# Three weight products moved from the matmul engine to the vector engine, and the last expert's down product cut in two halves

## The chip, the cores and the metric

The kernel runs on one core of one Trainium2 chip. TensorE (PE in the profile; its weight loads are PEld) multiplies, VectorE (DVE) and ScalarE (ACT) do elementwise work, GpSimd (POOL) little, SyncE (SP) issues nearly all DMAs. The metric is the device time of one execution in microseconds; lower is better.

## The reference, cut to what matters

Two transformer layers over 256 latent and 256 context tokens, width 1024. Each layer has six modulation vectors (adaLN) made from the conditioning vectors, a mixer and a feed-forward: layer 0 a dense SwiGLU, layer 1 eight experts of which each latent token uses two. Only the latent tokens leave.

```python
for i in range(DEPTH):                                   # DEPTH = 2
    mod_x = split(silu(c) @ ada_w[i] + ada_b[i], 6)      # 1024 x 6144 weights a layer
    mod_c = split(silu(c_ctx) @ ada_w[i] + ada_b[i], 6)
    hx = rms(x, norm1_w[i]) * (1 + mod_x[1]) + mod_x[0]
    hc = rms(ctx, norm1_w[i]) * (1 + mod_c[1]) + mod_c[0]
    y_x, y_c = mixer(hx @ w_in[i], hc @ w_in[i])
    x = x + mod_x[2] * (y_x @ w_out[i])
    h = rms(x, norm2_w[i]) * (1 + mod_x[4]) + mod_x[3]
    x = x + mod_x[5] * ffn(h)        # i=0: (silu(h@wg) * (h@wu)) @ wd, width 2816, also for ctx
                                     # i=1: sum over the token's 2 of 8 experts, width 3584
return rms(x, final_norm_w)
```

Context tokens use layer 1 only as far as the mixer, so of layer 1's vectors for `c_ctx` only the first two are used.

## The kernel before

The stages follow one another: layer 0's projection and mixer (to about 290 us), the dense feed-forward (FFN, about 300 to 690), layer 1's projection and mixer (to 870), the router, then the eight experts (908 to 1733) and the final norm.

**adaLN vectors.** `ada_w` of a layer is cut into three parts of two vectors, and each part into 8 loads of 1 MB, each as two tiles `araw` of 128x1024 numbers. `ada()` (L193 to 230) multiplies them on PE: for every load a group of 8 matmuls of 32 rows by 256 columns (L214), four of them side by side in the array, with the two conditioning vectors as two columns of `cz`. `sums` transposes and adds at a part's end. `adas` is a generator of such groups. Three of its parts, (0,1), (0,2) and (1,0), are woven into layer 0's mixer and two, (1,1) and (1,2), into layer 1's, at steps fixed in a list; layer 0's first part has loads of its own (tile `a`).

**Dense products.** `gemm` streams weights `raw` (512 KB, 4 KB to a partition) through two buffers. ACT rounds each to `wh` (L149) and DVE makes the rest `wl` (L150), five buffers of each, and PE does three matmuls a product (L335 to L337, 24 for a load). In the FFN DVE further multiplies gate and up (`f`, L841) and makes the rest of the rounded product (`fl`, L845). The FFN runs through the gate and up units of its first half, a first down product (`down(0)`), the second half, and `down(1)`.

**Experts.** `Ahead` loads an expert's weights through 16 buffers of 1 MB (`rawe`), on SP's queue and in order: gate and up (rows of 8 KB and of 6 KB to a partition), then the down weights `md` (14 loads of 8 KB to a partition). The first 8 loads are issued when the last dense weight is. A load's buffer is free when PE has used it. The tokens of an expert are gathered into 96 slots (3 groups of 32; the third group is left out by a branch where it is empty, as it is in the last block). `down()` accumulates y in 32 rows for each column half and parity; `scatter()` adds the parities (yc, ye: L1139, L1141), multiplies by `g2`, splits into `yh` and `yl` (L1144 to L1146), and matmuls with the one-hot `oht` (L1153, L1154) put the rows back to their tokens, to be added to `xt` (L1155). A scatter runs inside the next expert's work; the last one has no next.

**End.** After the last scatter an `If` (L1360) repeats the experts where more than 96 tokens chose one. Behind it come squares of `xt` (L1380), `rsqrt` (13 instructions on 128x2), the scaling by the norm's weights (L1387) and four output DMAs.

Of the kernel before, what the change touches and what calls it, by code (L numbers as in the profile page):

```python
# [9 lines left out]
F32 = mybir.dt.float32  # L10
# [26 lines left out]
WARM = (16, 4)  # L37

UPS, DOWNS = (0, 4, 8), (0, 4, 6, 10, 14)

# [34 lines left out]
def tile_hybrid(ctx: ExitStack, tc, a, tap=None):  # L75
# [171 lines left out]

    def mod(layer, i, j):

        return mods[layer, i // 2][:, (i % 2) * 8:(i % 2) * 8 + 8, j]  # L250
# [82 lines left out]

    def mm3(out, wh, wl, hh, hl, first, last):
        pe.matmul(out, wh, hh, start=first, stop=False)  # L335
        pe.matmul(out, wh, hl, start=False, stop=False)  # L336
        pe.matmul(out, wl, hh, start=False, stop=last)  # L337
# [452 lines left out]
    def add_gated(layer, i, m, o, lo, hi):  # L790
        for c0, c1, j in HALVES:
            if lo <= c0 < hi:
                dve.scalar_tensor_tensor(x[m][:, c0:c1], o[:, c0:c1], mod(layer, i, j)[:, m:m + 1], x[m][:, c0:c1],
                                         op0=ALU.mult, op1=ALU.add)
# [33 lines left out]
    def ffn(acc):  # L828
        with tc.tile_pool(name="ff", bufs=1, reuse_waits="tile") as FF:
# [3 lines left out]
            def evac(key, o, *_):  # L833
# [7 lines left out]
                dve.tensor_mul(f, o, hold.pop(m))  # L841
                H = FF.tile([128, TOK], F32R, tag="fh", name="fh", bufs=15)
                L = FF.tile([128, TOK], F32R, tag="fl", name="fl", bufs=15)
# [14 lines left out]
            yield from gemm(gu[:FCUT], hp, evac, KT, head=HEAD, halves=True)  # L858
            yield from gemm(down(0), f_rhs[0], evac_d, 11)
            yield from gemm(gu[FCUT:], hp, evac, KT)  # L860
# [28 lines left out]
    g = mixer(0, M0, adas(lambda: mx.pool, (0, 1), (0, 2), (1, 0)))  # L889
# [33 lines left out]
    p, g = g, mixer(1, mixer_pool("mix1"), adas(lambda: mx.pool, (1, 1), (1, 2)))  # L923
# [7 lines left out]
    class Ahead:  # L931


        def __init__(self, blocks):
            self.src, self.t, self.n = [], [], 0
            for up, down in blocks:
                for st in range(2):
                    self.src += [(lambda up=up, w=w, st=st, k=k: up(w, st, k), 4 * SCS[st]) for w in range(2)
                                 for k in range(KT)]
                self.src += [(lambda down=down, c=c: down(c), 2048) for c in range(14)]  # L940

        def issue(self, upto):
            while len(self.t) < min(upto, len(self.src)):
# [4 lines left out]
                nc.sync.dma_start(t[:, 0:c], src())  # L948
# [19 lines left out]
    loader = Ahead([weights(lambda: 0)] + [weights(lambda p=p: turn_of[p - 1]) for p in range(1, NE)])  # L968
# [135 lines left out]
    def prepare(poscol):  # L1104
# [19 lines left out]
        for t in range(2):  # L1124
            dve.tensor_scalar(oh[:, t, :], iota[:, 0:SLOTS], poscol(t), None, op0=ALU.is_equal)
        p = ps("mm", name="ohT")
# [32 lines left out]

    def experts(blocks, load, first, flag=None):  # L1160
# [5 lines left out]
        def groups(b, body, zero, first):  # L1166
# [356 lines left out]
```

## Time and profile before

| what | value |
|---|---|
| median of 3 runs | 1763.3 us (1760.02 to 1767.48) |
| the profiled execution | 1758.96 us, its span 1757.2 us |
| mean granted TensorE clock | 0.993 |
| PE busy | 1691.4 us (96%) |
| DVE busy | 602.8 us (34%) |
| ACT busy | 443.0 us (25%) |
| read from HBM | 469.36 MB |

The span is what the engines' instructions take; the execution's own time is 1.8 us more. A busy PE counts matmuls that overlap, so that a share near 100% says that it always had work, not that it ran at its peak.

### The profile page before, as it was taken

Reading aid. Unit: us, or ns where it says so; the run is one execution under the profiler, and the core shown is the slowest. Engines: PE = TensorE matmul, PEld = TensorE weight load, DVE = VectorE, ACT = ScalarE, POOL = GpSimd, SP = SyncE. Lnnn points to the kernel's source line nnn. Section 1 sums busy time; section 2 is a strip of 40 time slices with the busy share of each in tenths; the row PEclk is TensorE's granted clock in tenths of the full one; section 3 lists DMA queues with packets and bytes.
Section 4 is the critical chain, followed back from the end, with each engine's and each line's share of the span. In section 5 each row is a group of like instructions: output and inputs, shape, how many; then the busy total and the mean of one; then the engine's idle time right before and its main releaser. Section 6 shows DMA issues by size and latency. Waiting matters only on the chain. (4 is left out here: it accounts for less than half of the span.)

```text
span 1757.2 us, 31023 instructions
## 1 busy us (share of the span) xinstructions
PE 1691.4 (96%) x13008; PEld 1001.2 (57%) x13008; DVE 602.8 (34%) x1400; ACT 443.0 (25%) x863; POOL 19.4 (1%) x42
## 2 busy tenths in 40 slices
PE   6999999999999999999999999999999999999985
PEld 4875557988888889876675434334343443333431
DVE  5734665733333336647441210201211021210213
ACT  4543553433222223455430100100110010100101
POOL 1000000000000000000000000000000000000000
PEclk9999999999999999999999999999999999999997
DMA  8435552233333323355499999999999999999993
GB/s 326 148 111 196 176 175 71 77 104 96 96 96 96 96 96 109 108 188 197 166 391 417 420 417 420 414 384 420 412 419 418 419 420 416 420 417 420 419 418 150
DMA packets 84860, 472.68 MB, mean 269 GB/s; under 512 B 9424, under 2 KB 9808, under 8 KB 52704
## 3 DMA queue, kind: packets, MB, share of 16 engines
q1 hardware_dynamic: 84240, 469.36, 68.7%
q8 instruction: 117, 1.92, 0.4%
q0 software_dynamic: 176, 0.56, 0.1%
q10 hardware_dynamic: 288, 0.52, 0.1%
q14 instruction: 39, 0.32, 0.1%
HBM read 469.36 MB, written 1.05 MB: 268 GB/s over the span
## 5 line engine op out<-in xcount | busy, mean ns | idle before, releaser
L1186 PE MATMUL up<-rawe,G 128*32 128x512 f32 (+1 forms) x5120 | 496.6, 540 | 3.8 <-PEq L1170 2.7
L1186 PEld LDWEIGHTS up<-rawe,G 128*32 128x32 f32 x5120 | 184.5, 110 | 301.9 <-issue 270.8
L335 PE MATMUL mm<-hh,wh 128*128 128x512 f32 (+1 forms) x856 | 305.6, 360 | 4.0 <-ACT hh L330 4.0
L336 PE MATMUL mm<-hl,wh 128*128 128x512 f32 (+1 forms) x856 | 304.5, 356 | 0.0
L337 PE MATMUL mm<-hh,wl 128*128 128x512 f32 (+1 forms) x856 | 303.5, 355 | 0.0
L1216 PE MATMUL y<-rawe,e 128*32 128x512 f32 x2240 | 255.0, 597 | 11.5 <-DMA rawe<-in_md_dram 7.0
L149 ACT ACTIVATE wh<-raw 128x1024 fp32r<-128x1024 f32 x120 | 127.1, 1059 | 324.7 <-PE mm L336 290.6
L150 DVE TENSOR_TENSOR wl<-raw,wh 128x1024 fp32r<-128x1024 f32 x120 | 146.7, 1223 | 175.0 <-ACT wh L149 172.4
L335 PEld LDWEIGHTS mm<-hh,wh 128*128 128x128 f32 x856 | 161.0, 189 | 31.6 <-ACT hh L330 5.2
L1216 PEld LDWEIGHTS y<-rawe,e 128*32 128x32 f32 x2240 | 82.2, 110 | 168.9 <-issue 147.5
L336 PEld LDWEIGHTS mm<-hl,wh 128*128 128x128 f32 x856 | 161.8, 189 | 27.4 <-issue 5.2
L337 PEld LDWEIGHTS mm<-hh,wl 128*128 128x128 f32 x856 | 161.7, 189 | 23.3 <-issue 1.6
L1259 DVE TENSOR_TENSOR hid<-sg,up 128x512 f32<-128x512 f32 (+1 forms) x48 | 27.0, 616 | 288.1 <-PE up L1186 288.1
L1241 ACT ACTIVATE e<-hT 128x256 f32<-128x256 f32 (+1 forms) x48 | 17.1, 358 | 395.3 <-PE hT L1238 394.5
L335 PE MATMUL mm<-fh,wh 128*128 128x512 f32 (+1 forms) x209 | 74.5, 356 | 0.0
L336 PE MATMUL mm<-fl,wh 128*128 128x512 f32 (+1 forms) x209 | 74.3, 355 | 0.0
L337 PE MATMUL mm<-fh,wl 128*128 128x512 f32 (+1 forms) x209 | 74.3, 355 | 0.0
L1242 DVE COPY e<-hT 128x256 f32<-128x256 f32 (+1 forms) x48 | 18.3, 391 | 132.9 <-ACT e L1241 132.7
L214 PE MATMUL ada<-araw,cz 128*32 128x256 f32 x640 | 54.6, 390 | 8.7 <-DMA araw<-in_ada_dram 8.1
L1141 DVE TENSOR_TENSOR ye<-y,yc 32x512 f32<-32x512 f32 x48 | 32.7, 682 | 71.3 <-ACT yc L1139 70.6
L1255 ACT ACTIVATE sg<-up 128x512 f32<-128x512 f32 (+1 forms) x48 | 22.8, 544 | 134.0 <-PE up L1186 134.0
L1121 DVE TENSOR_SCALAR G<-ga,scale,shift 128x96 f32<-128x96 f32 x32 | 11.8, 371 | 114.3 <-ACT G L1123 114.3
(292 smaller groups left out, 1389.6 us busy)
## 6 DMA issues: line engine op xcount, KB each, us to landing
rawe<-in_md_dram SPq DMA_DIRECT2D x112, 1024.0 KB, 18.1
rawe<-in_g_dram SPq DMA_DIRECT2D x64, 1024.0 KB, 20.1
rawe<-in_u_dram SPq DMA_DIRECT2D x64, 1024.0 KB, 19.8
raw<-in_ws_dram SPq DMA_DIRECT2D x120, 512.0 KB, 3.6
rawe<-in_g_dram SPq DMA_DIRECT2D x64, 768.0 KB, 15.9
rawe<-in_u_dram SPq DMA_DIRECT2D x64, 768.0 KB, 14.9
araw<-in_ada_dram SPq DMA_DIRECT2D x80, 512.0 KB, 4.5
a<-in_ada_dram SPq DMA_DIRECT2D x8, 1024.0 KB, 11.4
```

What stands on the lines that cost most here:

```text
L149: act.activation(h, raw, AF.Copy)
L150: dve.tensor_sub(l, raw, h)
L214: pe.matmul(o[32 * g:32 * g + 32, 0:256], cz[:, kt, 16 - 2 * row:48 - 2 * row], t[:, z:z + 256], start=(first and kt < 4), stop=(last and ...
L335: pe.matmul(out, wh, hh, start=first, stop=False)
L336: pe.matmul(out, wh, hl, start=False, stop=False)
L337: pe.matmul(out, wl, hh, start=False, stop=last)
L1141: dve.tensor_add(ye[32 * s:32 * s + 32, n * 512:(n + 1) * 512], y[s][32 * n:32 * n + 32, :], yc[32 * n:32 * n + 32, :])
L1186: last = pe.matmul(o[s][32 * c:32 * c + 32, 0:sc], g[:, k, 32 * s:32 * s + 32], w[k][:, c * sc:(c + 1) * sc], start=(k == 0), stop=(k == K ...
L1216: last = pe.matmul(y[s][r:r + 32, :], e[s][:, 2 * i + par, :], w[i][:, par * 1024 + n * 512:par * 1024 + (n + 1) * 512], start=(i == 0), s ...
L1242: dve.tensor_copy(e[s][:, 16 * st + h:16 * st + 4 * n, :], z[:, h:])
L1255: act.activation(sg[s], o[:, 0:SCS[st]], AF.Silu)
L1259: dve.tensor_mul(hid[st, s], sg[s], o[:, 0:SCS[st]])
```

## The change

Layer 1's three adaLN parts leave both mixers and are made in the FFN by `ada_beside`: 48 loads of 512 KB, for each a multiply-add on DVE into running sums of 128x1024 (two of them for the vectors that context uses, else one; the first of eight is a copy on ACT), and when a vector's 8 loads are done, three steps into the next vector, 4 matmuls of 32x256 per sum add over the partitions. A step stands behind each of 48 units of `gemm`.

The down weights are laid out anew, so that a load of the last expert holds 512 columns of four row tiles. For all other experts a load stays 1 MB but is two runs of 4 KB for a partition where it was one of 8 KB. The last expert's down product makes columns 0 to 511 from its first seven loads and 512 to 1023 from the other seven, in parts of at most two loads at the end. The first half's scatter, its addition to `xt` and its squares run inside the second half. y stays in 128 rows (four row tiles side by side), is multiplied by `g2` and split as it is, and the one-hot matrix, repeated four times, adds the four in the scatter. The final norm stands before the `If`, whose body computes it again.

```diff
+    def ada_beside(pool):
...
+        def total(v, sums):
+            for j, t in enumerate(sums):
+                r = 6 * j + v
+                for g in range(4):
+                    pe.matmul(o[32 * g:32 * g + 32, 0:256], oz[:, 16 - r:48 - r], t[:, g * 256:(g + 1) * 256],
+                              start=(r == 0), stop=(v == 5), tile_position=(0, 32 * g), skip_group_check=True)
+        load(0)
+        yield
+        load(1)
+        o = ps("ax", name="adav")
+        for i in range(6 * KT):
+            v, k = divmod(i, KT)
+            if k == 0:
+                sums = [pool.tile([128, D], F32, tag="asum", name="asum", bufs=4) for _ in range(2 if v < 2 else 1)]
+            w = raw.pop(i)
+            for j, t in enumerate(sums):
+                c = cz[:, k, 16 + j:17 + j]
+                if k == 0:
+                    act.activation(t, w, AF.Copy, scale=c)
+                else:
+                    dve.scalar_tensor_tensor(t, w, c, t, op0=ALU.mult, op1=ALU.add)
+            load(i + 2)
+            if k == 2 and v:
+                total(v - 1, before)
+            if k == KT - 1:
+                before = sums
+            yield
+        total(5, before)
...
+            vectors = ada_beside(FF)
...
+            for part in (first, gemm(down(0), f_rhs[0], evac_d, 11), gemm(gu[FCUT:], hp, evac, KT)):
+                for _ in part:
+                    with tc.issue_after(latest["dve"]), tc.issue_after(latest["pe"]):
+                        step(vectors)
+                    yield
...
-    g = mixer(0, M0, adas(lambda: mx.pool, (0, 1), (0, 2), (1, 0)))
+    g = mixer(0, M0, adas(lambda: mx.pool, (0, 1), (0, 2)))
...
-    p, g = g, mixer(1, mixer_pool("mix1"), adas(lambda: mx.pool, (1, 1), (1, 2)))
+    p, g = g, mixer(1, mixer_pool("mix1"), iter(()))
...
-                lambda c: a["md"][bass.ds(e(), 1), c].squeeze(0))
+                lambda c: a["md"][bass.ds(e(), 1), c // 2, :, :, c % 2].squeeze(0),
+                lambda c: a["md"][bass.ds(e(), 1), c % 7, :, c // 7].squeeze(0))
...
+LASTS = ((0, 4, 6, 7), (0, 2, 4, 6, 7))
+LAST_GROUPS = (2, 0, 1)
...
+        def down_last(b, e, finish):
+            for n in range(2):
+                y = [ps(("y", "mm")[n], name="y") for _ in range(3)]
+                w = {}
+                for i0, i1 in zip(LASTS[n], LASTS[n][1:]):
...
+                    groups(b, body, zero, i0 == 0, LAST_GROUPS)
+                    if n and i0 == 0:
+                        with tc.issue_after(behind[0]):
+                            finish(0, half)
+                    yield
+                half = split_last(y, n)
+            with tc.issue_after(behind[0]):
+                finish(1, half)
...
+    def split_last(y, n):
...
+        for i, s in enumerate(LAST_GROUPS):
+            dve.tensor_mul(u[s], y[s], g2[:, n * 512:(n + 1) * 512])
+            act.activation(h[s], u[s], AF.Copy)
+            for z in {0: (), 1: LAST_GROUPS[0:1], 2: LAST_GROUPS[1:]}[i]:
+                dve.tensor_sub(l[z], u[z], h[z])
...
+    def finish(n, half, oht, wcol):
...
+            if n and z == LAST_GROUPS[0]:
+                with tc.issue_after(last.ins):
+                    idle(WARM[2])
+        s = slice(n * 512, (n + 1) * 512)
+        for t in range(2):
+            dve.scalar_tensor_tensor(xt[:, t, s], p[t], wcol(t), xt[:, t, s], op0=ALU.mult, op1=ALU.add)
+            act.activation(xf[t][n], xt[:, t, s], AF.Square, accum_out=vn[:, t, n:n + 1])
+        for t in range(2):
+            dve.tensor_mul(xf[t][n], xt[:, t, s], fn[:, s])
```

Three places show how instructions move. The first is PE at the end of layer 1's mixer; `av` and `sc` are products of the mixer, `ada<-araw` the adaLN products, `mm` the next dense product. Before:

```order
L740 MATMUL av<-PT,vt_5760 64x256 x2
L740 MATMUL av<-PT,vt_5761 64x256 x2
L740 MATMUL av<-PT,vt_5762 64x256 x2
L715 MATMUL sc<-akz_5763,qa_5768 128x512
L214 MATMUL ada<-araw,cz 32x256 x8
L715 MATMUL sc<-akz_5764,qa_5768 128x512 x2
L335 MATMUL mm<-hh_89,wh 128x256
```

and there in the changed kernel:

```order
L803 MATMUL av<-PT,vt_5874 64x256 x2
L803 MATMUL av<-PT,vt_5875 64x256 x2
L803 MATMUL av<-PT,vt_5876 64x256 x2
L778 MATMUL sc<-akz_5877,qa_5882 128x512
L778 MATMUL sc<-akz_5878,qa_5882 128x512 x2
L398 MATMUL mm<-hh_89,wh 128x256
```

The rows of the mixer keep their order here, and the groups between them are gone. The second place is DVE in the FFN's first half, where `f` is the product of gate and up, `fl` its rest and `wl` the rest of a weight. Before:

```order
L841 TENSOR_TENSOR f<-mm,sg 128x512
L150 TENSOR_TENSOR wl<-raw,wh 128x1024
L845 TENSOR_TENSOR fl<-f,fh 128x512
L150 TENSOR_TENSOR wl<-raw,wh 128x1024
L841 TENSOR_TENSOR f<-mm,sg 128x512
```

and in the changed kernel, `asum` being the running sums:

```order
L904 TENSOR_TENSOR f<-mm,sg 128x512
L289 SCALAR_TENSOR_TENSOR asum<-araw,cz,asum 128x1024
L908 TENSOR_TENSOR fl<-f,fh 128x512
L289 SCALAR_TENSOR_TENSOR asum<-araw,cz,asum 128x1024 x3
L153 TENSOR_TENSOR wl<-raw,wh 128x1024 x2
L904 TENSOR_TENSOR f<-mm,sg 128x512
```

Between two `f`, which are two units of `gemm` apart, stand four multiply-adds more, and both `wl` follow them. The third place is DVE at the end of the last expert. Before:

```order
L1141 TENSOR_TENSOR ye<-y,yc 32x512 x6
L1144 TENSOR_TENSOR ye<-ye,g_7406 96x1024
L1146 TENSOR_TENSOR yl<-ye,yh 96x1024
L1155 SCALAR_TENSOR_TENSOR xt<-scat,wet,xt 128x512 x4
L1359 TENSOR_LOAD ovf
L1360 COMPARE_AND_BRANCH
```

and in the changed kernel, for the second half of the columns, `lu` being y times `g2` (the first, of the empty third group, depends on nothing late), `xf` the stream times the norm's weights and `fv` the sum of squares:

```order
L1257 TENSOR_TENSOR lu<-y,g_7308 128x512 x2
L1260 TENSOR_TENSOR yl<-lu,yl 128x512
L1257 TENSOR_TENSOR lu<-y,g_7308 128x512
L1260 TENSOR_TENSOR yh<-lu,lh 128x512 x2
L1279 SCALAR_TENSOR_TENSOR xt<-scat,wet,xt 128x512 x2
L1282 TENSOR_TENSOR xf<-xt,fn 128x512 x2
L1543 SCALAR_TENSOR_TENSOR fv<-vn,fv 128x2
```

Six additions of parities are gone, the rest is by 512 columns, and the product with the norm's weights stands ahead of the sum of squares. The branch of the `If`, before ahead of the norm, now stands behind it.

## Rows read from the trace of the kernel before

**Rows 1.** Windows: start:end, us, busy us (x) of PE, PEld, DVE, ACT, POOL; PEclk, DMA, GB/s

```profile
420.00:640.00 220.00, 220.00 (x972) 182.19 (x971) 73.83 (x84) 58.09 (x69) 0.00 (x0) 1.00 0.31 98
...
1000.00:1700.00 700.00, 691.78 (x6805) 270.86 (x6794) 112.77 (x208) 61.22 (x129) 0.00 (x0) 1.00 1.01 416
...
1733.00:1757.00 24.00, 5.02 (x18) 2.32 (x8) 14.20 (x29) 5.40 (x12) 0.00 (x0) 0.57 0.12 45
```

**Rows 2.** Windows, the three stretches with layer 1's adaLN products

```profile
225.00:270.00 45.00, 43.20 (x300) 22.48 (x299) 26.91 (x91) 23.85 (x74) 0.00 (x0) 1.00 0.51 175
760.00:800.00 40.00, 39.45 (x317) 28.59 (x315) 19.06 (x75) 17.78 (x41) 1.20 (x3) 1.00 0.69 236
800.00:862.00 62.00, 58.90 (x407) 33.77 (x406) 41.65 (x127) 35.25 (x90) 3.79 (x5) 1.00 0.52 169
```

**Rows 3.** Windows, the same stretches, tile araw alone: PE, PEld, PEclk, DMA, GB/s

```profile
225.00:270.00 45.00, 10.02 (x128) 2.62 (x128) 1.00 0.51 175
760.00:800.00 40.00, 8.44 (x106) 2.29 (x106) 1.00 0.69 236
800.00:862.00 62.00, 13.83 (x152) 3.58 (x150) 1.00 0.52 169
```

**Rows 4.** Timeline of PE in layer 0: start us, us, engine, line, instruction

```profile
134.39 0.40 PE L335 MATMUL mm<-hh,wh 128*128 128x512 f32 x1
134.71 0.64 PE L214 MATMUL ada<-araw,cz 128*32 128x256 f32 x8
135.28 0.50 PE L336 MATMUL mm<-hl,wh 128*128 128x512 f32 x1
```

**Rows 5.** Waits of all engines, 800 to 862: us in total, times, longest

```profile
ACT PT L731 <- PE pT L728: 10.8, 7, 3.0
...
PE ada L214 <- DMA araw<-in_ada_dram: 2.1, 5, 0.8
```

**Rows 6.** Waits of DVE in the FFN, 320 to 640

```profile
DVE wl L150 <- ACT wh L149: 103.8, 33, 4.2
DVE f L841 <- PE mm L337: 68.8, 21, 3.4
```

**Rows 7.** Lines of DVE, form by form: duration ns min/median/max

```profile
L150 DVE TENSOR_TENSOR wl<-raw,wh x120: 1206/1225/1227, 17.9 to 881.8; 128x1024 fp32r<-128x1024 f32 x120
...
L331 DVE SCALAR_TENSOR_TENSOR hl<-u,mod,hh x48: 470/479/486, 24.3 to 707.9; 128x256 fp32r<-128x256 f32 x48
...
L841 DVE TENSOR_TENSOR f<-mm,sg x22: 691/692/692, 347.3 to 628.8; 128x512 f32<-128x512 f32 x22
...
L1155 DVE SCALAR_TENSOR_TENSOR xt<-scat,wet,xt x32: 740/743/751, 1014.9 to 1744.5; 128x512 f32<-128x512 f32 x32
```

**Rows 8.** Windows: rows of 8 KB, of 6 KB, and mixer and dense weights (4 KB)

```profile
966.00:1028.00 62.00, 61.52 (x547) 23.99 (x543) 12.86 (x24) 7.12 (x14) 0.00 (x0) 1.00 1.01 419
...
1036.00:1058.00 22.00, 21.99 (x264) 9.03 (x260) 3.15 (x6) 2.41 (x6) 0.00 (x0) 1.00 1.02 417
...
797.00:799.00 2.00, 1.84 (x19) 1.23 (x18) 1.90 (x15) 0.02 (x1) 0.00 (x0) 1.00 1.03 406
```

**Rows 9.** Timeline of all engines from the last weight load on

```profile
1731.95 1.92 PE L1216 MATMUL y<-rawe,e 128*32 128x512 f32 x16 [0.54 <-SPq L1360]
...
1733.71 4.18 DVE L1141 TENSOR_TENSOR ye<-y,yc 32x512 f32<-32x512 f32 x6 [20.55 <-ACT yc L1139]
...
1742.37 2.88 DVE L1155 SCALAR_TENSOR_TENSOR xt<-scat,wet,xt 128x512 f32<-128x512 f32 x4 [0.89 <-PE scat L1154]
...
1743.84 0.63 PE L1154 MATMUL scat<-yl,oht 128*128 128x512 f32 x1
1745.82 0.63 ACT L1380 ACTIVATE fsq<-xt 128x512 f32<-128x512 f32 x1 [5.58 <-DVEq L1360]
...
1748.40 0.16 DVE L1381 TENSOR_TENSOR fv<-vn 128x2 f32<-128x2 f32 x1 [3.15 <-ACT fsq L1380]
...
1750.97 2.74 DVE L1387 SCALAR_TENSOR_TENSOR xt<-xt,fr,fn 128x512 f32<-128x512 f32 x4
```

More of the change, by code (lines that the diff above doesn't have):

```diff
@@ L336, in mm3 @@
         pe.matmul(out, wh, hl, start=False, stop=False)
-        pe.matmul(out, wl, hh, start=False, stop=last)
+        latest["pe"] = pe.matmul(out, wl, hh, start=False, stop=last).ins
     base = [0]
@@ L857, in ffn @@
             down = lambda i: [(0, (i, m)) for m in range(KT)]
-            yield from gemm(gu[:FCUT], hp, evac, KT, head=HEAD, halves=True)
-            yield from gemm(down(0), f_rhs[0], evac_d, 11)
-            yield from gemm(gu[FCUT:], hp, evac, KT)
+            vectors = ada_beside(FF)
+            first = gemm(gu[:FCUT], hp, evac, KT, head=HEAD, halves=True)
+            for _ in range(2 * KT):
+                next(first)
+                yield
[3 more added lines that the diff above has]
+                        step(vectors)
+                    yield
+            run(vectors)
             yield from gemm(down(1), f_rhs[1], evac_d, 11, head=HEAD, tail=TAILD)
@@ L931, in tile_hybrid, with __init__ @@
     class Ahead:
-        def __init__(self, blocks):
+        def __init__(self, blocks, halves=False):
             self.src, self.t, self.n = [], [], 0
-            for up, down in blocks:
+            for i, (up, down, half) in enumerate(blocks):
                 for st in range(2):
@@ L939, in __init__ @@
                                  for k in range(KT)]
+                down = half if halves and i == len(blocks) - 1 else down
                 self.src += [(lambda down=down, c=c: down(c), 2048) for c in range(14)]
@@ L1271, in experts @@
                 run(u)
-            y = [ps("y", name="y") for _ in range(3)]
-            u = down(b, y, e)
+            last = flag and b == len(blocks) - 1
+            if last:
+                u = down_last(b, e, lambda n, half: finish(n, half, oht, blocks[b][1]))
+            else:
+                y = [ps("y", name="y") for _ in range(3)]
+                u = down(b, y, e)
             step(u)
@@ L1279, in experts @@
                 with tc.issue_after(behind[0]):
[L1280 removed]
+                    nxt = prepare(blocks[b + 1][0], flag and b + 1 == len(blocks) - 1)
+                    if flag and b + 1 == len(blocks) - 1:
+                        with tc.issue_after(behind_oh[0]), tc.issue_after(behind_oh[1]):
+                            over.append(nc.values_load_multi_w_load_instructions(ovf[0:1, 0:1], min_val=0, max_val=1,
+                                                                                      bass_reorder=False)[1][0])
                     if flags:
@@ L1283, in experts @@
             run(u)
-            pending = scatter(y, oht, blocks[b][1])
-        run(pending)
+            pending = None if last else scatter(y, oht, blocks[b][1])
+        if pending:
+            run(pending)
     p1.close()
@@ L1299, in tile_hybrid, with xf_tiles @@
             act.activation(xt[:, t, :], ht[:, t, :], AF.Copy)
+    fn = XP.tile([128, D], F32, name="fn")
+    xf, over = [], []
+    def xf_tiles():
+        a_ = XP.tile([128, D], F32, tag="ye", name="xf", bufs=1)
+        xf[:] = [[a_[:, 0:512], a_[:, 512:]], [XP.tile([128, 512], F32, tag="yc", name="xf", bufs=2) for _ in range(2)]]
+    vn = RS.tile([128, 2, 2], F32, name="vn")
     post, wet = sm("post"), sm("wet")
```

144 lines of the change are left out of this document (109 added, 35 removed).

## The prediction

> **What bounds the kernel now.** I read the windows first, because the changed parts lie in stretches with different limits. In the FFN PE is busy for all of 420 to 640 us while DVE works a third of the time and DMA a third [rows 1]. From 1000 to 1700 the DMA share is 1.01 at 416 GB/s and PE is busy for 691.78 of 700 us: the experts' stream of weights sets the pace and PE is just fast enough [rows 1]. In the last 24 us PE works 5.02 us at a granted clock of 0.57, and a chain over DVE and ACT sets the end [rows 1]. So a microsecond saved on PE ahead of the experts brings the stream forward by a microsecond, one added to a weight load comes back many times, and the tail is worth what its chain becomes.
>
> Then I read the three stretches that lose work. PE is the busiest engine in each: 43.20 of 45, 39.45 of 40, 58.90 of 62 us [rows 2]. The adaLN products alone take 10.02, 8.44 and 13.83 us of it, 32.3 us for 384 of their matmul records, which are 48 groups of 8 [rows 3]. The timeline gives the same price by another way: with a group between them two dense matmuls stand 135.28 - 134.39 = 0.89 us apart [rows 4], without one 220/972 = 0.226 us [rows 1]; 0.66 us a group, 32 us for 48.
>
> **Part 1, PE in the mixers.** What of the 32.3 us is gained depends on what is next. From 760 to 800, DVE and ACT are busy 19.06 and 17.78 us of 40 [rows 2], well below what remains of PE (31 us): I take all 8.4 us. From 800 to 862, PE keeps 45.1 us and DVE has 41.65 [rows 2], and the chains between the engines are near: ACT waits 10.8 us for PE's transposes there, which then come earlier, and PE waits 2.1 us for the removed loads [rows 5]. I take 70% of 13.83, 9.7 us, with bounds of 4 and of 13.83 + 2.1. In layer 0, PE keeps 33.2 of 45 us against DVE's 26.91 [rows 2]: 70% of 10.02, 7.0 us, bounds 3 and 10. Three sums with six transposes, counted as slots of 0.226 us [rows 1], are 1.4 us (bounds 0 and 1.4). Together 26.5 us, bounds 16 and 36.
>
> **Part 1, PE in the FFN.** Eight sums of four matmuls of 32x256 are half a group of L214 each: 0.33 us, or 0.66 us if the entry to such a group is most of its price [rows 4]. With the two transposes behind ACT's copy at the end I take +5 us, bounds 3 and 8; PE has no slack there [rows 1], so this is paid in full. Net for both: -21.5 us, bounds -8 and -33.
>
> **Part 1, the work that hides.** 48 steps bring 56 multiply-adds of 128x1024 and 8 copies on ACT. One multiply-add is 479 ns at 256 and 743 ns at 512 elements [rows 7], so 743 + 2 x 264 = 1271 ns at 1024; `wl` with as many elements is 1225 [rows 7]. The tight place is the first 16 steps, with two sums. A unit is 24 matmuls, 5.43 us, so a pair of gate and up is 10.9 us of PE [rows 1]. DVE has for a pair `f` at 0.692, `fl`, counted like `f`, and two `wl` at 1.225 [rows 7]: 3.8 us; four multiply-adds add 5.1, so 8.9 of 10.9 us. It fits, and the waits agree: DVE stood idle 103.8 us for ACT's `wh` and 68.8 us for PE [rows 6], 172.6 us for 56 x 1.27 = 71 us. Queued behind a multiply-add are `fl` and the next `wl`; five buffers of `wl` stand between DVE and PE, 27 us of work. ACT has 58.09 busy of 220 us [rows 1], and 8 copies are nothing. The 48 loads stand on SP's queue among the dense weights'; with 512 KB each 5.43 us they add what the dense stream has, so the DMA share goes from 0.31 to some 0.62 [rows 1]. I cost all this at nothing; if the cover is gone, the third rival has the price.
>
> **Part 2, the down weights in runs of 4 KB.** 98 loads of seven experts change; the last expert's 14 are one run again. Rows of 8 KB move at 419 GB/s and rows of 6 KB at 417 [rows 8]. A fixed price for each run, through these two, puts 4 KB at 413 GB/s: 2.54 us for 1 MB instead of 2.50, +3.5 us for 98. The nearest row with 4 KB to a partition at a full share is 406 GB/s, over 2 us only [rows 8]: +7.9 us. The far bound is the FFN's dense stream, also 4 KB: 98 GB/s at a share of 0.31 [rows 1], 316 GB/s scaled up, which would be 3.32 us a load and +80 us. That stream has only two buffers and starts and stops, so I keep it for a rival and take +4 us, bounds 0 and 8.
>
> The Trainium skill, page "DMA: Bandwidth & Descriptors", section "Specifications", puts the smallest transfer that reaches full rate at 512 B; by that, runs of 4 KB would cost nothing, and the sum would be 4 us lower. The rows of 8 and 6 KB do not quite agree (419 and 417, both far above that size) [rows 8].
>
> **Part 2, the tail.** From the start of the last load's matmuls at 1731.95 to the span's end at 1757.2 are 25.25 us [rows 9]. The new chain, from that start: the matmuls take 1.92 us as before, the first group's being done at about 1.1. Then DVE has five operations of 128x512 in a row (two products with `g2`, three rests; that of the empty third group is early) at 0.69 us as `f` [rows 7]: to 4.6. Four scatter matmuls remain, 0.9 us at full clock: 5.5 (at the low clock, 0.63 us for each [rows 9], 7.1). Two additions to `xt` at 0.743 [rows 7]: 7.0. The last square, 0.63 us [rows 9], lies beside two products of 0.69 on DVE: 8.4. Twelve small operations at (1750.97 - 1748.40)/13 = 0.198 us [rows 9]: 10.8. Two scalings on each of ACT and DVE, 0.69 each: 12.2. The outputs then need what they need now, from 1753.71 to 1757.2 [rows 9]: 3.5 us, so 15.7. What goes is the parities (4.18), the 0.57 us between the last addition and the first square, three of four squares, and half of the scatter and additions [rows 9]. The first half's work, some 10 us of DVE, lies inside seven loads of 2.5 us. I take -9 us, bounds -6 and -11.
>
> **Sum.** -21.5 + 4 - 9 = -26.5 us on an execution of 1758.96 us, so 1732.5. That execution lies 4.3 us under the median of the runs; against 1763.3 I predict 1737 us.
>
> **The rivals.**
> 1. *The runs of 4 KB are slow*, which ends on the other side. A load takes 3.32 us as the dense stream suggests [rows 1]: -21.5 + 80 - 9 = +49.5, 1813 us. It decides from the point where a load takes 30.5/98 = 0.31 us more, a rate of 373 GB/s. Against it stand 417 and 406 [rows 8]. Chance 0.05.
> 2. *The mixers are bound by their chains*, not by PE: only the 8.4 us of 760 to 800 are gained, less 5 in the FFN. For it speaks DVE's 41.65 beside PE's 45.1 [rows 2]; against it, that ACT waits for PE there [rows 5]. -3.4 + 4 - 9 = -8.4, 1755 us. Chance 0.13.
> 3. *DVE becomes the bound in the first 16 steps*, if a multiply-add costs over (10.9 - 3.8)/4 = 1.76 us. At twice a `wl`, 2.45 us, a pair takes 13.6 us, and seven pairs (the others' are copies on ACT) 19 us more: 1756 us. The row of 743 ns for 512 speaks against it [rows 7]. Chance 0.05.
> 4. *The tail does not shrink* (the new scatter or the outputs wait for something that I do not see): 1746 us. Chance 0.10.
> 5. *All of the PE time comes back*, with the loads' waits, and runs of 4 KB cost nothing: -33 - 11 = -44, 1719 us. For it speaks a PE busy over 95% in all three stretches [rows 2]. Chance 0.10.
>
> **How the numbers follow.** My forecast has 0.57, with a range of its own of 1728 to 1746. The range of 1722 to 1755 takes in the fourth case and the near part of the others, and leaves out the first, half of the second, third and fifth: about 2 in 10. What a measurement can tell from no change is 0.5%, 8.8 us: faster is under 1754.5. Forecast, fourth and fifth case and a third of the second make 0.81, the rest of the second and the third 0.13; slower, the first case and what I may have missed of its kind, has 0.06.
>
> **What would show it.** Between 760 and 862 PE's busy time falls by 22 us, and the first expert product starts some 21 us earlier than 908; if it is under 10 earlier, the second case holds, and PE's waits in the mixer have grown. In the FFN PE stays at 100% and DVE rises by about 71 us; a PE that waits for `wl` is the third case. In a window of down loads at full share the rate reads 413 GB/s; under 373 is the first. From the last load's matmuls to the span's end are 16 us. I am wrong if the stream's start does not move with PE, if the rate under `md` falls, or if the tail has a new wait.

## The result, and the profile after

The changed kernel takes 1744.87 us (1743.95 to 1746.69, 4 runs) against 1765.22 us (1760.02 to 1767.48) for the kernel before: 0.9895, 95% interval 0.9875 to 0.9916, some 20 us faster. I had forecast 1737, 26 us faster.

The trace of one execution (1746.69 us, span 1744.8) answers to [rows 1] and [rows 2]. Windows, with the columns of those rows:

```profile
180.00:250.00 70.00, 61.93 (x382) 32.91 (x381) 41.31 (x147) 36.05 (x115) 0.00 (x0) 0.97 0.33 110
420.00:640.00 220.00, 220.00 (x1002) 179.09 (x1001) 114.99 (x129) 60.81 (x72) 0.00 (x0) 1.00 0.56 176
760.00:800.00 40.00, 37.26 (x259) 32.58 (x258) 26.47 (x90) 23.95 (x52) 2.41 (x5) 0.99 0.30 95
800.00:862.00 62.00, 58.07 (x339) 41.07 (x338) 40.39 (x132) 32.36 (x88) 3.13 (x5) 0.95 0.11 42
800.00:810.00 10.00, 9.66 (x30) 6.37 (x29) 7.98 (x21) 3.80 (x11) 2.60 (x4) 0.70 0.11 43
1000.00:1700.00 700.00, 684.57 (x6704) 265.56 (x6706) 111.03 (x211) 60.35 (x129) 0.00 (x0) 0.99 1.02 413
1728.00:1745.00 17.00, 3.59 (x15) 2.11 (x14) 7.52 (x22) 3.60 (x8) 0.00 (x0) 0.69 0.18 66
```

The first window has this row in the kernel before:

```profile
180.00:250.00 70.00, 66.12 (x455) 35.02 (x454) 44.00 (x157) 37.72 (x118) 0.73 (x1) 1.00 0.56 186
```

The reader sees three things. PE now has longer pauses in the mixers, and there the granted clock is below 1.00; in the kernel before it was 1.00 in every one of these mixer windows (this row and [rows 2]). In the FFN DVE has 41 us more to do in 220 us and PE still has no pause. In the experts' stream the rate is 413 where it was 416. DVE's wait for ACT's `wh` in the FFN, from 320 to 640, which answers to [rows 6], has shrunk from 103.8 us:

```profile
DVE wl L153 <- ACT wh L152: 45.1, 25, 4.2
```

Where each stage begins is read from three tiles. `xall` is first written where layer 0's mixer ends, `f` marks the FFN, `up<-rawe` the experts' up products (first to last) and `y<-rawe` their down products. First the kernel before, by tile (duration ns min/median/max, first and last start):

```profile
L793 DVE SCALAR_TENSOR_TENSOR xall<-mm,mod,xall x56: 473/478/485, 294.0 to 895.6; 128x256 f32<-128x256 f32 x56
L1186 PE MATMUL up<-rawe,G x5120: 482/550/617, 908.6 to 1697.8; 128*32 128x512 f32 x99, 128*32 128x384 f32 x98
L1216 PE MATMUL y<-rawe,e x2240: 589/592/1062, 961.8 to 1733.3; 128*32 128x512 f32 x187
```

then the changed kernel, the same tiles and lines:

```profile
L856 DVE SCALAR_TENSOR_TENSOR xall<-mm,mod,xall x56: 473/478/485, 289.9 to 879.8; 128x256 f32<-128x256 f32 x56
...
L904 DVE TENSOR_TENSOR f<-mm,sg x22: 691/692/692, 343.1 to 629.5; 128x512 f32<-128x512 f32 x22
...
L289 DVE SCALAR_TENSOR_TENSOR asum<-araw,cz,asum x56: 1273/1278/1282, 358.6 to 630.1; 128x1024 f32<-128x1024 f32 x56
...
L1310 PE MATMUL up<-rawe,G x5120: 482/550/617, 892.8 to 1688.0; 128*32 128x512 f32 x99, 128*32 128x384 f32 x98
...
L1370 PE MATMUL y<-rawe,e x224: 589/592/1061, 1689.6 to 1727.0; 128*32 128x512 f32 x112
```

| stage, from these rows (us) | before | after | change | forecast |
|---|---|---|---|---|
| to the first `xall` | 294.0 | 289.9 | -4.1 | -7.0 |
| first `xall` to first `up` | 614.6 | 602.9 | -11.7 | -14.5 |
| of that, first to last `f` | 281.5 [rows 7] | 286.4 | +4.9 | +5 |
| first to last `up` | 789.2 | 795.2 | +6.0 | +4 |
| last `up` to last `y` | 35.5 | 39.0 | +3.5 | 0 |
| last `y` to the span's end | 23.9 | 17.8 | -6.1 | -9 |

(-14.5 is 8.4 + 9.7 + 1.4 less 5.) The two traces are 12.4 us apart, the medians 20: the traced execution of the kernel before (1758.96) is shorter than all of its timed runs, and the changed one (1746.69) is the longest of its own. The experiments show where such differences arise.

The end of the changed kernel, timeline of all engines, which answers to [rows 9]:

```profile
1718.08 5.36 PE L1370 MATMUL y<-rawe,e 128*32 128x512 f32 x48
...
1725.71 1.92 PE L1370 MATMUL y<-rawe,e 128*32 128x512 f32 x16 [0.17 <-PEq L1294]
...
1726.84 0.69 DVE L1257 TENSOR_TENSOR lu<-y,g 128x512 f32<-128x512 f32 x1 [0.45 <-PE y L1370]
...
1731.22 1.41 DVE L1279 SCALAR_TENSOR_TENSOR xt<-scat,wet,xt 128x512 f32<-128x512 f32 x2 [1.04 <-PE scat L1272]
...
1734.02 0.15 DVE L1543 SCALAR_TENSOR_TENSOR fv<-vn,fv 128x2 f32<-128x2 f32 x1
...
1736.38 1.33 ACT L1551 ACTIVATE xf<-xf,fr 128x512 f32<-128x512 f32 x2 [3.00 <-DVE fr L336]
1736.38 0.88 DVE L1549 TENSOR_SCALAR xf<-xf,fr 128x512 f32<-128x512 f32 x2
1736.89 1.10 SPq L1552 DMA_DIRECT2D out_dram<-xf  x2
1737.13 0.95 ACTq L1552 DMA_DIRECT2D out_dram<-xf  x2
```

From the start of the last load's products the chain went as worked out: `xt` done at 6.9 us (7.0 in the sum), `fv` at 8.3 (8.4), the scaling's start at 10.7 (10.8) and end at 12.0 (12.2). But the outputs and the end then took 7.1 us, not 3.5. And the last `y` starts late for another reason than a load: PE's wait before it is 0.17 us, behind the branch that leaves out the empty third group (L1294).

One more thing made PE late in the last expert. With the first four loads it waits three times for a load, 1.32 to 1.43 us each, each time after 1.06 or 1.07 us of products. Below are the next 40 products, the window around them, and the same 40 products in the kernel before, where the waits are 1.34, 1.41 and 1.20 us and four short products with zeros stand ahead of the last:

```profile
1696.99 6.12 PE L1370 MATMUL y<-rawe,e 128*32 128x512 f32 x40 [1.42 <-DMA rawe<-in_md_dram]
1697.00:1703.00 6.00, 6.00 (x40) 1.38 (x40) 0.00 (x0) 0.00 (x0) 0.00 (x0) 0.72 1.00 418
...
1706.76 4.50 PE L1216 MATMUL y<-rawe,e 128*32 128x512 f32 x40 [1.20 <-DMA rawe<-in_md_dram]
```

The same 40 products take 1.6 us more at the lower clock.

### The profile page after: what moved, and what is told of

Read it like the earlier page. It is cut to its first block, busy times and chain, and to the rows that moved or that the text cites. A ratio compares the mean times of both kernels' runs of the same rounds, so it can differ in the third digit from the quotient of the medians.

```text
span 1744.8 us, 30522 instructions
## 1 busy us (share of the span) xinstructions
PE 1676.9 (96%) x12710; PEld 996.8 (57%) x12712; DVE 668.6 (38%) x1471; ACT 449.9 (26%) x874; POOL 19.4 (1%) x42
## 3 DMA queue, kind: packets, MB, share of 16 engines
q1 hardware_dynamic: 96784, 469.36, 69.7%
## 5 line engine op out<-in xcount | busy, mean ns | idle before, releaser
L1340 PE MATMUL y<-rawe,e 128*32 128x512 f32 x2016 | 228.8, 599 | 5.6 <-DMA rawe<-in_md_dram 4.2
L1340 PEld LDWEIGHTS y<-rawe,e 128*32 128x32 f32 x2016 | 74.2, 110 | 146.0 <-issue 132.1
L289 DVE SCALAR_TENSOR_TENSOR asum<-araw,cz,asum 128x1024 f32<-128x1024 f32 x56 | 70.5, 1278 | 0.0
L1244 DVE SCALAR_TENSOR_TENSOR xt<-scat,wet,xt 128x512 f32<-128x512 f32 x28 | 19.1, 745 | 79.5 <-PE scat L1243 79.5
```

The lines of the kernel that those rows point to most:

```text
L289: dve.scalar_tensor_tensor(t, w, c, t, op0=ALU.mult, op1=ALU.add)
L1244: dve.scalar_tensor_tensor(xt[:, t, s], p, wcol(t), xt[:, t, s], op0=ALU.mult, op1=ALU.add)
L1340: last = pe.matmul(y[s][r:r + 32, :], e[s][:, 2 * i + par, :], w[i][:, n * 1024 + par * 512:n * 1024 + (par + 1) * 512], start=(i == 0), s ...
```

## The experiments

**The first part alone.** The kernel before with `ada_beside`, nothing of the last expert.

```diff
-    g = mixer(0, M0, adas(lambda: mx.pool, (0, 1), (0, 2), (1, 0)))
+    g = mixer(0, M0, adas(lambda: mx.pool, (0, 1), (0, 2)))
...
+            vectors = ada_beside(FF)
...
-    p, g = g, mixer(1, mixer_pool("mix1"), adas(lambda: mx.pool, (1, 1), (1, 2)))
+    p, g = g, mixer(1, mixer_pool("mix1"), iter(()))
```

> Only the first part of the change: layer 1's adaLN vectors on VectorE in the FFN; down weights and the last expert as in the kernel before. In the changed kernel's trace the first expert product starts 15.8 us earlier than before (892.8 against 908.6). Theory: all of that comes from this part, so it starts there again and the end is 15 to 16 us earlier than in the kernel before, some 0.991 of its time, with the mixers' ends 4 us (layer 0) and 15 us (layer 1) earlier in sum and the FFN 5 us longer. Rival: part of it is owed to run-to-run differences, or the stream of expert weights gives it back; then the experts start earlier but the end moves by less than 8 us (0.996 or more).

1741.9 us, 0.9881 (0.9859 to 0.9902). Up products from 892.9 to 1682.2, so the stream takes 789.3 us, as before, and the last `y` comes 35.4 us after, as before. The first theory holds: all of the gain is here, and the rest of the change adds nothing to it (3 us less gain, if anything).

**The second part alone.**

```diff
+            last = flag and b == len(blocks) - 1
+            if last:
+                u = down_last(b, e, lambda n, half: finish(n, half, oht, blocks[b][1]))
...
+    o["md"] = np.ascontiguousarray(w).reshape(8, 7, 128, 2, 2, 1024)
```

(with all that belongs to these, and layer 1's products in the mixers as before)

> Only the second part: the down weights laid out anew and the last expert in halves; adaLN as before. Theory from the two traces: the seven down products with runs of 4 KB cost 6 us, the last expert's product 3.5 us more, the tail is 6 us shorter; in sum 3 us slower than before, a ratio of about 1.002. Rival, as the prediction had it: 4 us for the runs and 9 us off the tail, 5 us faster, 0.997.

1765.97 us, 1.0013 (0.9999 to 1.0027): no gain, as the first theory says, not 0.997. In its trace the stages of this part cost 8.1 us in the stream (797.3) and 3.1 before the last `y`, and give 7.3 behind it: 3.9 us lost, where the changed kernel loses 3.4. Its trace shows something else too: its front is that of the kernel before, yet `xall` starts at 296.6, not 294.0. PE's timeline there:

```profile
139.35 0.40 PE L340 MATMUL mm<-hh,wl 128*128 128x512 f32 x1
141.49 1.08 PE L217 MATMUL ada<-araw,cz 128*32 128x256 f32 x8 [1.75 <-DMA araw<-in_ada_dram]
142.50 0.80 PE L338 MATMUL mm<-hh,wh 128*128 128x512 f32 x1
143.10 0.63 PE L339 MATMUL mm<-hl,wh 128*128 128x512 f32 x1
...
145.09 0.39 PE L338 MATMUL mm<-hh,wh 128*128 128x512 f32 x1
```

An adaLN group waited 1.75 us for its load, and the matmuls behind it took 0.63 us instead of 0.40: the granted clock is 0.83 in the window from 140 to 150, against 1.00 in the kernel before. So this late load in layer 0's mixer cost its wait and then a stretch at the lower level of the clock, 1.2 GHz.

**The layout of the down weights alone.**

```diff
-                lambda c: a["md"][bass.ds(e(), 1), c].squeeze(0))
+                lambda c: a["md"][bass.ds(e(), 1), c // 2, :, :, c % 2].squeeze(0))
...
-    o["md"] = np.ascontiguousarray(w).reshape(8, 14, 128, 2048)
+    o["md"] = np.ascontiguousarray(w).reshape(8, 7, 128, 2, 2, 1024)
```

> The kernel before with nothing changed but the layout of the down weights: each load of all eight experts is two runs of 4 KB to a partition instead of one of 8 KB. Theory: the runs cost 0.05 us a load, so the time grows by 5 to 7 us (ratio 1.003 to 1.004) and windows within the down loads read 413 GB/s or a little less against 419 before. Rival: runs of 4 KB cost nothing (413 has another cause, such as waits for buffers), ratio 1.000. The rate of the FFN's dense stream would make 1.05.

1772.74 us, 1.0054 (1.0034 to 1.0075), some 10 us more, above the 5 to 7 of the theory. The stream takes 1709.8 - 915.3 = 794.5 us, 5.3 more than before. Its windows within down loads:

```profile
972.00:996.00 24.00, 23.69 (x208) 10.54 (x202) 3.60 (x12) 2.71 (x7) 0.00 (x0) 1.00 1.03 412
1184.00:1206.00 22.00, 22.00 (x237) 9.14 (x229) 1.67 (x4) 0.55 (x2) 0.00 (x0) 1.00 1.03 409
```

The share is 1.03, so the queue does not stand idle; the runs themselves are slower. Of the rest of this trace 6.7 us lie in front, where nothing was edited (`xall` at 298.4, `up` at 915.3, with a granted clock of 0.83 from 160 to 170), and 1.7 us between the last `up` and the last `y` (37.2 against 35.5). So of the 10 us 5.3, or 7.0 with the last expert, lie where the layout was changed.

**The kernel before once more,** without an edit.

> The kernel before, unchanged, for a second trace: its executions lie between 1759 and 1767 us, and the one shown is the fastest. Theory: they differ in the experts' stream (waits for loads, 1000 to 1733 us), while everything ahead of the first expert product at 908.6 repeats within 1 us. Rival: they differ in the front, or in the clock.

1758.83 us. `xall` starts at 294.2, `up` runs from 908.5 to 1697.7, the last `y` at 1733.2: within 0.2 us of the first trace. So these two traces do not tell why other executions take up to 1769 us. What the four traces with this front show together is that it differs ahead of the experts: `up` starts at 908.6, 908.5, 911.9 and 915.3 (mean 911.1) with layer 1's products in the mixers. With the products in the FFN seven traces (no filling, below) have 892.8, 892.9, 891.2, 891.8, 892.6, 893.3 and 888.9 (mean 891.9). The difference is 19.2 us, not 15.8; at `xall` it is 295.8 against 288.9, 6.9 us.

**Down weights held twice.** The first seven experts read runs of 8 KB from `md`, the last one its halves from a second copy, `md2`.

```diff
-                lambda c: a["md"][bass.ds(e(), 1), c // 2, :, :, c % 2].squeeze(0),
-                lambda c: a["md"][bass.ds(e(), 1), c % 7, :, c // 7].squeeze(0))
+                lambda c: a["md"][bass.ds(e(), 1), c].squeeze(0),
+                lambda c: a["md2"][bass.ds(e(), 1), c % 7, :, c // 7].squeeze(0))
```

> The changed kernel with the down weights held twice in memory: the first seven experts read them in runs of 8 KB as in the kernel before, the last expert in halves as in the change. Theory: the seven down products lose their 5.5 to 6 us again (792.4 us from the first to the last expert's up product become 786 to 787 by this trace's clock, as in the runs with the old layout), so the time is 5 to 7 us under the changed kernel's, about 1739 us, ratio 0.986 of before. Rival: the stream is slower for another reason than the runs (the last expert's structure, the clock), and the time stays at 1745, ratio 0.989.

1739.83 us, 0.9864 (0.9849 to 0.9879). (The 792.4 in the expectation is misread; the rows above give 795.2 for the changed kernel.) Up products from 891.2 to 1680.8, 789.6 us: the whole cost of the runs is back, and the window from 948 to 972 reads

```profile
948.00:972.00 24.00, 23.69 (x207) 10.62 (x203) 3.59 (x12) 2.71 (x7) 0.00 (x0) 1.00 1.02 421
```

where the changed kernel's from 950 to 974 reads

```profile
950.00:974.00 24.00, 23.69 (x207) 10.59 (x203) 3.59 (x12) 2.72 (x7) 0.00 (x0) 1.00 1.02 412
```

**Smaller parts in the last expert.**

```diff
-LASTS = ((0, 4, 6, 7), (0, 2, 4, 6, 7))
+LASTS = ((0, 2, 4, 6, 7), (0, 2, 4, 6, 7))
```

> The changed kernel with one number list changed: the last expert's first half of the columns in parts of 2, 2, 2 and 1 loads where it was 4, 2 and 1. Theory: in the last down product PE, not the loads, ends last (it works without a pause from 1697 to 1727.6 while the last load has landed by about 1721), because a part's second group waits for all four loads and then lags; with parts of two loads some 2 us of that lag go, and the clock does not fall at 1697: the last load's products start 2 to 4 us earlier, ratio to the changed kernel 0.998 to 0.999. Rival: the loads end last, and nothing moves.

1743.71 us, 0.9885 (0.987 to 0.99). From the last `up` (1687.2) to the last `y` (1724.4) are 37.2 us instead of 39.0 (38.4 to 40.5 in the eight traces with the old parts): 1.8 us went, and 1.7 us remain over the kernel before. The ratio alone could not have told it. The theory named two causes, the lag and the clock, and the run changed both: the window in which the changed kernel has 0.72 reads

```profile
1697.00:1703.00 6.00, 5.57 (x49) 1.53 (x44) 0.00 (x0) 0.00 (x0) 0.00 (x0) 1.00 1.02 425
```

By size the clock (1.6 us above) accounts for nearly all of the 1.8; the two were not taken apart.

**Idle matmuls in the mixers, two at each place.**

```diff
+    def fill(steps, n):
+        o = ps("ax", name="fill")
+        for i in range(steps):
+            for _ in range(n):
+                pe.matmul(o, zf[:, 0:128], zf, start=True, stop=True)
+            yield
...
-    p, g = g, mixer(1, mixer_pool("mix1"), iter(()))
+    p, g = g, mixer(1, mixer_pool("mix1"), fill(32, 2))
```

(and `fill(16, 2)` behind layer 0's groups)

> The changed kernel with idle matmuls (two of 128x512 in 16-bit, some 0.45 us) at the 48 places in the mixers where the removed products stood: 16 in layer 0, 32 in layer 1; they depend on nothing and their result is not used. In the changed kernel the granted clock fell to half three times in the mixers, for 13.6 us in all. Theory: the missing part of the gain lies in these falls, which cost up to 6.8 us; with PE kept busy the clock stays at full speed and the experts start 2 to 6 us earlier in spite of 21 us of idle matmuls, most of which lie in gaps. Rival: the mixers are held by the chains between the engines (the second case of the prediction) and the falls cost nothing on the path; then the experts start at the same time or later, by up to 10 us.

1754.13 us, 0.9943 (0.993 to 0.9957), 9 us slower than the changed kernel. The clock stayed at 1.00 in the mixers, but `up` starts at 901.6, 8.8 us later. The rival has the time, but not the reason: the mixer itself became shorter. Its last product `av`, first the changed kernel, then this one (`xall` starts at 289.9 in both):

```profile
L803 PE MATMUL av<-PT,vt x160: 379/379/689, 189.9 to 857.2; 128*64 128x256 f32 x160
...
L817 PE MATMUL av<-PT,vt x160: 379/379/431, 192.0 to 855.0; 128*64 128x256 f32 x160
```

The loss lies behind. The first product of layer 1's dense part stood between the mixer's last ones in the changed kernel; here 27 idle matmuls stand there, and it comes 9.9 us later. PE's timeline, first the changed kernel, then this one:

```profile
846.32 0.68 PE L398 MATMUL mm<-hh,wh 128*128 128x256 f32 x1
...
844.97 2.32 PE L259 MATMUL fill<-zf 128*128 128x512 bf16 x10
...
856.22 0.47 PE L412 MATMUL mm<-hh,wh 128*128 128x256 f32 x1
```

The last dense weight was also issued later, at 861.7 instead of 855.4 and behind the first eight expert loads instead of ahead of them. By these rows the idle matmuls in the mixer's pauses cost nothing, and those that took the place of the dense products cost the 9 us.

**One at each place.** Against the run with two:

```diff
-    p, g = g, mixer(1, mixer_pool("mix1"), fill(32, 2))
+    p, g = g, mixer(1, mixer_pool("mix1"), fill(32, 1))
```

(and `fill(16, 1)` in layer 0)

> The changed kernel with one idle matmul (about 0.23 us) at the 48 places in the mixers where the run with two had 0.45 us, so 11 us of them instead of 22. Two cost 9 us in time, with the falls of the clock in the mixers gone. Theory: PE's time in the mixers is worth some 40 to 70% of itself, whatever it does; then half of the filling costs half, 4 to 5 us, less what the clock gives back: 1746 to 1750 us. Rival: what costs is the order of the work that the filling changed, and the falls of the clock are the missing part of the gain; then one matmul keeps the clock at nearly no cost, 1740 to 1743 us.

1741.78 us, 0.987 (0.9853 to 0.9886), 3 us faster than the changed kernel by the medians, though the intervals overlap: my theory falls and the rival's time holds. Windows of this kernel, against 0.99 and 0.95 above:

```profile
760.00:800.00 40.00, 39.21 (x252) 31.96 (x254) 27.88 (x89) 23.46 (x54) 3.43 (x6) 1.00 0.30 93
800.00:862.00 62.00, 61.26 (x389) 44.90 (x390) 41.88 (x134) 33.61 (x89) 2.08 (x3) 1.00 0.20 79
```

From the first `xall` (285.5) to the first `up` (886.5) are 601.0 us, where all traces of the changed front without filling have 602.9 to 603.2. The mixer's part of that shows in all three kernels with filling: from the last `f` to the last `av` they take 225.5 to 225.8 us, the seven without it 227.7 to 228.1. So some 2 us of the missing gain in layer 1 come back with the clock, whether one or two idle matmuls keep it up. That it is the clock is read from the windows; no run raised the clock without the filling. The other 4.4 us of this trace lie ahead of `xall`, where a trace without filling (below) has nearly the same, 285.9; they are not shown to come from the filling. With one matmul at each place the first dense product comes at 840.0, 10.9 us ahead of the last `av`, as in the changed kernel (846.3 and 857.2); that is what the run with two lost.

**The outputs in one queue.**

```diff
-                (nc.scalar, nc.sync)[n].dma_start(a["out"][t * 128:(t + 1) * 128, n * 512:(n + 1) * 512], z)
+                nc.sync.dma_start(a["out"][t * 128:(t + 1) * 128, n * 512:(n + 1) * 512], z)
```

> The changed kernel with all four output transfers on SP's queue, one after the other, where they are on two queues at once. From the last scaling to the span's end it takes 7.1 us where the kernel before takes 3.5: the transfers land 2.8 to 4.7 us after their issue against 2.1 to 2.2 before. Theory: four transfers issued within 0.8 us share the way out and slow each other; in one queue they are issued over 1.1 us and the last lands earlier or at the same time, a change of -1 to 0 us. Rival: it is the branch behind the transfers and the waits that end a kernel; then landing times fall to 2.1 us and the span's end does not move.

1744.47 us, 0.9893 (0.9874 to 0.9912): no change, within what theory and rival both allow. Issues are at 1737.5 to 1739.2, landings 2.7 to 3.9 us behind; from the scaling's start to the span's end are 8.0 us (8.4 in the changed kernel). The queue is not the cause.

**Without the branch at the end.** This leaves out the pass for experts with more than 96 tokens, branch and body.

```diff
-    with tc.If(over[0] > 0):
...
-        final()
```

> The changed kernel without the pass for experts that more than 96 tokens chose: the branch at the program's end and its body are left out, so an input that overflows would not be computed in full (this one does not overflow). In the changed kernel 8.4 us lie between the end of the last small operation (1736.4) and the span's end, before it was 6.2. Theory: the branch, now behind the outputs, and the instructions that are fetched around it while the outputs are written, cost 2 us; without it the end comes 1.5 to 2.5 us earlier, 6 to 6.5 us after the small operations. Rival: the outputs are bound by their own writing (1 MB at some 380 GB/s), and the end moves by less than 0.7 us.

1741.12 us, 0.9866 (0.9849 to 0.9882). In the changed kernel the branch (L1557) has these entries, among others, which stand on the engines' own queues:

```profile
L1557 SPq EVENT_SEMAPHORE  x8: 17/17/17, 1742.8 to 1743.3; - x8
...
L1557 PEldq COMPARE_BRANCH  x1: 3888/3888/3888, 1730.2 to 1730.2; - x1
```

Without it, the end:

```profile
1732.61 1.33 ACT L1551 ACTIVATE xf<-xf,fr 128x512 f32<-128x512 f32 x2 [3.00 <-DVE fr L336]
...
1733.12 1.10 SPq L1552 DMA_DIRECT2D out_dram<-xf  x2
```

with a span of 1739.0: 6.4 us from the scaling's start, where the changed kernel has 1744.8 - 1736.4 = 8.4 and the kernel before 1757.2 - 1751.0 = 6.2 [rows 9]. So this pair gives 2.0 us for the branch behind the outputs, as the theory said. The other traces with that branch take 7.2 to 8.5 us (mean of nine 8.0), so that it is 0.9 to 2.1 us, 1.6 in the mean, against one trace without it. Where it lies the DMA columns tell, first the changed kernel, then this one, then the kernel before:

```profile
1740.00:1741.00 1.00, 0.00 (x0) 0.00 (x0) 0.00 (x0) 0.00 (x0) 0.00 (x0) 0.50 0.60 217
1741.00:1742.00 1.00, 0.00 (x0) 0.00 (x0) 0.00 (x0) 0.00 (x0) 0.00 (x0) 0.50 0.03 12
...
1736.00:1737.00 1.00, 0.00 (x0) 0.00 (x0) 0.00 (x0) 0.00 (x0) 0.00 (x0) 0.50 0.80 289
1737.00:1738.00 1.00, 0.00 (x0) 0.00 (x0) 0.00 (x0) 0.00 (x0) 0.00 (x0) 0.50 0.02 8
...
1755.00:1756.00 1.00, 0.00 (x0) 0.00 (x0) 0.00 (x0) 0.00 (x0) 0.00 (x0) 0.50 0.42 158
```

By these shares the last bytes of the outputs move at about 1740.6, 1736.8 and 1755.4, that is 4.2, 4.2 and 4.4 us after the scaling's start; behind them the changed kernel takes another 4.2 us, this one 2.2 and the kernel before 1.8. PE's 3.9 us at the branch begin at 1730.2 and end before the outputs are issued; they are not what stands at the end.

Of the 5.8 us between the two traces nearly all of the rest is the front: the experts start at 888.9 here, at 892.8 there. The medians, 3.8 us apart with intervals that overlap, could not have told the branch from that.

**Two edits together: weights held twice and smaller parts.** The lines of both:

```diff
-LASTS = ((0, 4, 6, 7), (0, 2, 4, 6, 7))
+LASTS = ((0, 2, 4, 6, 7), (0, 2, 4, 6, 7))
...
+                lambda c: a["md"][bass.ds(e(), 1), c].squeeze(0),
+                lambda c: a["md2"][bass.ds(e(), 1), c % 7, :, c // 7].squeeze(0))
```

> The changed kernel with the down weights held twice, as in the run of that name, and the last expert's first half in parts of 2, 2, 2 and 1 loads: the two edits that each came out faster. Theory: they act in different places (the seven down products' stream; PE's lag in the last one), so they add up: 5 us and 1 us, about 1738.5 us, 0.985 to 0.986 of the kernel before. Rival: with the faster stream the loads of the last expert land earlier still and PE's lag in it grows, so that the parts give nothing or more than 1 us: 1736 or 1740.

1739.68 us, 0.9857 (0.9841 to 0.9874), no faster than the layout alone. Its last `up` to last `y` is 37.3 us, as with the parts alone, where the layout alone had 38.4: 1.1 us, which the times of these runs cannot tell.

**Weights held twice and one idle matmul.** Only the new lines (`fill` as above, and `fill(16, 1)` in layer 0):

```diff
+    p, g = g, mixer(1, mixer_pool("mix1"), fill(32, 1))
...
+                lambda c: a["md"][bass.ds(e(), 1), c].squeeze(0),
+                lambda c: a["md2"][bass.ds(e(), 1), c % 7, :, c // 7].squeeze(0))
```

> The changed kernel with both edits that were worth something: the down weights held twice (runs of 8 KB for the first seven experts) and one idle matmul at the 48 places in the mixers where the products stood. Theory: they act in different stages and add up: 5 us in the stream, 3 us in the mixers, about 1736 to 1737 us, ratio 0.984 of the kernel before; the clock does not fall in the mixers and the stretch from the start of layer 0's output product to the first expert product takes 601 us where the changed kernel takes 603. Rival: the 3 us of the filling came from layer 0's loads falling well by chance; then it gives 1739 to 1740, the same as the layout alone.

1736.35 us (1733.23 to 1743.71, 5 runs), 0.9858 (0.9832 to 0.9884), the lowest median of all; the interval overlaps with that of the layout alone. In its trace first `xall` (287.9) to first `up` (888.8) is 600.9 us and the stream 1678.5 - 888.8 = 789.7: both parts of the theory show, in their own stages.

## Why the prediction was right, point by point

The direction and the reason were right: PE's time ahead of the experts brings the stream forward one for one, and DVE had room in the FFN. The time came out 6 us above the sum, but the traces show the terms further off than that: the stages of the first two traces add up to -12.4 us, over all traces to some -16, where the sum had -26.5. Of these last 10 us 6.4 lie in the tail, the rest in layer 1's mixer and the runs of 4 KB. That the medians are 20 us apart comes in part from executions that have no trace, so that the nearness of the number is in part luck.

- *PE in layer 0's mixer, -7.0.* In the two first traces 4.1, over the traces together 6.9. Two of the four traces of the old front have a stretch at the lower clock there, one of them behind a load that landed late; without these two it is 5.2. All of this lies within the bounds of 3 and 10. Whether the share of 70% is right no run tells, and 128, 106 and 152 records of [rows 3] are 386, not 384, which changes nothing.
- *PE in layer 1's mixer and the sums, -19.5.* The stretch gave 11.7 + 4.9 = 16.6. I took a share of PE's busy time because chains between the engines would hold the rest. The runs show that some 2 us of what was missing come back when idle matmuls keep the clock up, which fell when the removed products left pauses: 0.70 in the window from 800 to 810 of the changed kernel, where PE was busy for 7.26 of the 10 us before. That step was missing; the second rival (only 8.4 us gained) is refuted. One sign was badly chosen: PE's busy time between 760 and 862 fell by 3.0 us (98.35 to 95.33), not by 22, because the work behind moved into the fixed window.
- *PE in the FFN, +5.* 4.9 by `f`. The multiply-add took 1278 ns (1271 in the sum), and DVE's waits took it in, for `wh` 45.1 us where they were 103.8 [rows 6]. The third rival is refuted.
- *Runs of 4 KB, +4.* 5.3 to 6.8 in seven traces with this layout (8.1 in an eighth, the second part alone). The rate is 409 to 412 GB/s; the fixed price for each run had given 413, and the 406 of [rows 8] was nearly right too. The queue's packets rise from 84240 to 96784, by 98 x 128, so that each run is one packet. The first rival (316) is refuted. The Trainium skill, page "DMA: Bandwidth & Descriptors", section "Specifications", would have 512 B suffice for the full rate; this case disagrees, 421 against 412 GB/s at 8 KB and 4 KB. Another section of that page, "Why small descriptors are slow (HBM only)", gives each packet a fixed price of about 3 cycles beside its 32-byte beats, which by an estimate from it (259 cycles for 8 KB, 262 for two runs of 4 KB) is 1.2%; the measured loss is 2.1%, the same way and larger.
- *The tail, -9.* This is the step that failed. Its chain of operations came out to 0.2 us. Two things were not in it. The last `y` starts 3.5 us later after the last `up`: PE has the first half's scatter to do between the second half's products (3.4 us, 1714.72 to 1718.08) and loses 1.6 us to the lower clock at 1697, so that it and not the load ends last. (The smaller parts gave 1.8 us back; the scatter's share is read from the timeline, since no run takes it out.) I had named what DVE does there and called it hidden, and had not counted PE. And I let the outputs "need what they need now"; the branch, which I counted as moved out of the way, went behind them and costs 0.9 to 2.1 us there; and though the scalings became 1.4 us shorter (2.74 to 1.33), the last bytes of the outputs move 4.2 us after their start instead of 4.4: issued closer together, the four land 2.8 to 4.7 us after issue instead of 2.1 to 2.2. The tail gave 6.1 - 3.5 = 2.6 us, less than the 6.0 that its layout costs the stream.

Of the rivals the fourth, a tail that does not shrink (1746 us), is closest to what happened, in its number and in its kind. What stays open: the sum of the stages by mean fronts is -19.2 + 6.0 + 3.5 - 6.1 = -16 us, and the medians say -20 with an interval from -22 to -15; which stage of the untraced executions makes the difference no trace here shows.

## What to carry to other kernels

Count a moved piece of work on every engine that it touches: the first half's scatter was hidden on VectorE and paid for on TensorE. A layout that one block out of eight needs is paid by all eight; a second copy of the weights gave the 5 us back. When filler work leaves an in-order engine, look at the granted clock as well as at the waits: a very small filling can be worth more than the emptiness. But see where it ends up: idle matmuls in pauses were free here, and 27 of them in the place of the next stage's first products cost 9 us.

## What the runs showed of the hardware

- Loads of 1 MB in two runs of 4 KB to a partition move at 409 to 412 GB/s, in one run of 8 KB at 419 to 421, with the DMA share at 1.01 to 1.03 in both.
- One wait of 1.75 us of PE was followed by matmuls of 0.63 us instead of 0.40 for about 3 us.
- Three waits of PE of 1.32 to 1.43 us, with 1.06 or 1.07 us of products between them, were followed by 6 us with a mean granted clock of 0.72; 40 products took 6.12 us instead of 4.50.
- With idle matmuls in its pauses a mixer kept the granted clock at 1.00 and took some 2 us less, with one (11 us in all) as with two (22 us).
- The branch over the overflow pass took 3.9 us of PE's queue; standing behind the outputs it lengthened the end by 0.9 to 2.1 us.
- Two traces of one kernel agreed to 0.2 us in every stage, while kernels with the same front differed by up to 6.8 us at the first expert product.
